# A memory norm done feature-major: statistics by a DRAM round trip, GpSimd in place of TensorE transposes

## The chip, the cores and the metric

The kernel runs on one core of a Trainium2 chip. The metric is the device time of one execution in microseconds (us). Before the change it is 1298.52 us, the median of three runs (1297.15 to 1299.23).

## The reference

Two layers of a decoder trunk on 256 tokens of width 1024, all in fp32. Cut to what matters here:

```python
def layer_norm(x, g, b):
    mu = xf.mean(-1, keepdims=True)
    var = jnp.square(xf - mu).mean(-1, keepdims=True)
    return (xf - mu) * lax.rsqrt(var + LN_EPS) * g + b

def hybrid_layer(x, mem_n, ...):
    h = layer_norm(ALPHA * x + 0.5 * swiglu(x, ffn1_w_gu, ffn1_w_down), ln_g[0], ln_b[0])
    ...
    o_xa = memory_cross_attention(xa_q, mem_n, w_mem_kv)     # k, v = split(mem_n @ w_mem_kv)
    ...

def reference(x, mem, mem_ln_g, mem_ln_b, ...):
    mem_n = layer_norm(mem, mem_ln_g, mem_ln_b)              # (256, 1024), once for both layers
    for l in range(2):
        x = hybrid_layer(x, mem_n, ...)
```

What is left out of a layer is gated DeltaNet, sliding-window attention, the gated merge with its output projection and norm, and the second SwiGLU with its norm. The product mem_n @ w_mem_kv needs mem_n with its features on the 128 partitions, as TensorE contracts over partitions.

## The kernel before

Every fp32 operand of a large product is split into a high part (ScalarE's cast to fp32r, "hi") and the rest (VectorE's subtraction, "lo"): `split`, lines 115 to 117. Weights come as one stream of units of 512 KB (`unit`, line 99): SyncE loads a unit into one of three raw buffers, ScalarE casts it into one of five whi buffers, VectorE subtracts into one of five wlo buffers. A product is then three matmuls: hi by hi, hi by lo, lo by hi (line 126 holds every matmul).

The first SwiGLU runs as *steps* f = 2 to 21 (`Ffn.rest`, line 369). A step computes 128 gate and 128 up features for all 256 tokens (`shares`, line 167): two units of weights, 32 matmuls in eight quads, two PSUM banks out of four. So a step can't begin before the banks of the step two back are read, by ScalarE's copies (L183) and VectorE's additions (L184). Then follow ScalarE's SiLU (L372 before), VectorE's product (L374 before) and a split into the tile u. After step 21 comes the down projection, then the norm of the stream, and `memory_kv` (line 448), which multiplies the normalised memory by w_mem_kv.

The norm of the memory is slipped between the steps of the first layer by `memory_T` (line 423), whose functions are called behind given steps: 11 loads gain and bias, broadcast over partitions (gB, bB); 13 and 15 load 128 memory tokens each into a tile pp, norm it on VectorE (`layernorm` with no src) and have TensorE transpose it (`to_T`: eight 128x128 transposes a tile, through PSUM), with ScalarE and VectorE splitting the result into w0 to w3; 16 writes these four tiles to DRAM (mdr), from where the second layer reads them back.

The order on each engine is set by a scheduler at build time and is then fixed: an engine runs its rows one after the other, and a row that waits holds all behind it. Loads are kept in program order on SyncE. The casts and subtractions of weight units have a priority that moves them ahead.

Of the kernel before, what the change touches and what calls it, by code (L numbers as in the profile page):

```python
# [14 lines left out]
ALU = mybir.AluOpType  # L15
AX = mybir.AxisListType

P = 128
# [19 lines left out]
@with_exitstack  # L38
def tile_trunk(ctx, tc, x, xT, mem, wst, lnp, memln, cvw, rows, cst, out):
    nc = tc.nc  # L40
# [232 lines left out]
    def layernorm(y, gB, bB, eps, src=None, fin=None, sizes=(512, 512)):  # L273
# [14 lines left out]

        if src:
            nc.scalar.activation(rs, mv[:, 1:2], AF.Sqrt, bias=epsc[:, eps:eps + 1])  # L290
            nc.vector.reciprocal(rs, rs)
            nc.vector.scalar_tensor_tensor(rt, mv[:, 1:2], epsc[:, eps:eps + 1], rs, op0=ALU.add, op1=ALU.mult)
            nc.vector.scalar_tensor_tensor(rt, rt, -0.5, rs, op0=ALU.mult, op1=ALU.mult)
            nc.vector.scalar_tensor_tensor(rs, rt, 1.5, rs, op0=ALU.add, op1=ALU.mult)
# [128 lines left out]
    def memory_T(mT, l):  # L423

        got = {}
        flat = lambda t: t.rearrange("p k t -> p (k t)")

        def again():
            mT.extend(T(pu, [P, 4, S], f"w{i}", F32R) for i in range(4))
            for i, t in enumerate(mT):  # L430
                nc.gpsimd.dma_start(flat(t), mdr[i])

        def keep():
            for i, t in enumerate(mT):
# [12 lines left out]

# [672 lines left out]
```

## Time and profile before

| | us |
|---|---|
| median of the runs | 1298.52 |
| the profiled execution, its own time | 1298.02 |
| its span in the trace | 1296.2 |
| TensorE busy | 1277.9 (99%) |
| VectorE busy | 888.4 (69%) |
| ScalarE busy | 708.5 (55%) |
| GpSimd busy | 77.2 (6%) |

In the profile PE is TensorE's matmuls, PEld its weight loads, DVE VectorE, ACT ScalarE, POOL GpSimd, SP SyncE. A row of a timeline gives the start, the length, the engine, the source line and operation, what is written <- what is read, and in brackets the idle time before it and what ended that. Times count from the start of the span. Names of tiles stand without buffer numbers: t<-acc is the pair of a step's banks being read, whi and wlo are weight units, pp the memory tile, w the four tiles of normalised memory.

### The profile page before, as it was taken

Reading aid. Unit: us, or ns where it says so; the run is one execution under the profiler, and the core shown is the slowest. Engines: PE = TensorE matmul, PEld = TensorE weight load, DVE = VectorE, ACT = ScalarE, POOL = GpSimd, SP = SyncE. Lnnn points to the kernel's source line nnn. Section 1 sums busy time; section 2 is a strip of 40 time slices with the busy share of each in tenths; the row PEclk is TensorE's granted clock in tenths of the full one; section 3 lists DMA queues with packets and bytes.
Section 4 is the critical chain, followed back from the end, with each engine's and each line's share of the span. In section 5 each row is a group of like instructions: output and inputs, shape, how many; then the busy total and the mean of one; then the engine's idle time right before and its main releaser. Section 6 shows DMA issues by size and latency. Waiting matters only on the chain.

```text
span 1296.2 us, 20444 instructions
## 1 busy us (share of the span) xinstructions
PE 1277.9 (99%) x7832; PEld 1116.2 (86%) x7832; DVE 888.4 (69%) x1430; ACT 708.5 (55%) x1177; POOL 77.2 (6%) x135
## 2 busy tenths in 40 slices
PE   8999999999999999999999999999999999999997
PEld 6888889999878888888888888899988788888886
DVE  6787556796647777665677674759867388777645
ACT  6656444666674546554455654456656654565541
POOL 0000000102311000000000000000033100000000
PEclk9999999999999999999999999999999999999999
DMA  7867564654533636555665555556453256455553
GB/s 266 276 210 244 193 229 128 220 174 135 161 131 130 228 129 211 191 185 192 228 222 200 188 186 192 199 175 201 163 165 131 98 182 224 149 194 194 189 189 111
DMA packets 68577, 240.25 MB, mean 185 GB/s; under 512 B 8160, under 2 KB 9312, under 8 KB 68480
## 3 DMA queue, kind: packets, MB, share of 16 engines
q1 hardware_dynamic: 66176, 232.53, 53.1%
q0 software_dynamic: 2304, 6.43, 1.8%
q8 instruction: 61, 1.00, 0.3%
q14 instruction: 36, 0.29, 0.1%
HBM read 235.64 MB, written 3.28 MB: 184 GB/s over the span
## 4 chain that ended last, share of the span: by engine, by line
PE 89%; DVE 4%; DMA 4%; ACT 2%; issue 1%; SPq 0%; DVEq 0%; ACTq 0%
PE acc L126 78%; PE at L126 4%; DMA raw<-in_wst_dram 3%; PE sm L126 3%; PE sm L129 1%; ACT whi L116 1%; DVE wlo L117 1%; PE acc L340 1%; PE acc L337 1%; DMA pp<-in_mem_dram 1%; PE acc L338 1%; PE at L129 1%; DVE bnst L282 0%; DVE u L117 0%; DVE h L301 0%
## 5 line engine op out<-in xcount | busy, mean ns | idle before, releaser
L117 DVE TENSOR_TENSOR wlo<-raw,whi 128x1024 fp32r<-128x1024 f32 (+2 forms) x403 | 487.4, 1214 | 308.7 <-ACT whi L116 307.2
L116 ACT CAST whi<-raw 128x1024 fp32r<-128x1024 f32 (+2 forms) x403 | 414.4, 1033 | 366.7 <-DMA raw<-in_wst_dram 99.0
L126 PE MATMUL acc<-hT,whi 128*128 128x512 f32 (+1 forms) x1952 | 524.9, 357 | 0.0
L126 PEld LDWEIGHTS acc<-hT,wlo 128*128 128x128 f32 x1616 | 304.6, 189 | 56.0
L126 PE MATMUL acc<-hT,wlo 128*128 128x256 f32 x1616 | 347.6, 279 | 0.0
L126 PEld LDWEIGHTS acc<-hT,whi 128*128 128x128 f32 x1952 | 299.8, 190 | 0.2
L126 PE MATMUL acc<-whi,u 128*128 128x512 f32 (+1 forms) x800 | 246.7, 373 | 0.0
L126 PEld LDWEIGHTS acc<-whi,u 128*128 128x128 f32 x800 | 150.1, 188 | 27.7 <-DVE t L184 1.2
L126 PE MATMUL acc<-whi,hT 128*128 128x512 f32 (+1 forms) x544 | 168.4, 380 | 5.6 <-ACT whi L116 5.6
L126 PE MATMUL acc<-wlo,u 128*128 128x512 f32 (+1 forms) x400 | 148.4, 371 | 0.0
L126 PEld LDWEIGHTS acc<-whi,hT 128*128 128x128 f32 x544 | 100.6, 189 | 23.7 <-ACT whi L116 5.6
L126 PE MATMUL acc<-wlo,hT 128*128 128x512 f32 (+1 forms) x272 | 101.9, 375 | 0.0
L126 PEld LDWEIGHTS acc<-wlo,u 128*128 128x128 f32 x400 | 75.5, 189 | 12.2
L372 ACT ACTIVATE t<-t 128x256 f32<-128x256 f32 x80 | 33.4, 417 | 60.4 <-DVE t L184 59.9
L184 DVE TENSOR_TENSOR t<-t,acc 128x256 f32<-128x256 f32 x160 | 59.9, 415 | 0.0
L126 PEld LDWEIGHTS acc<-wlo,hT 128*128 128x128 f32 x272 | 51.5, 190 | 8.2 <-DVE wlo L117 0.9
L183 ACT COPY t<-acc 128x256 f32<-128x256 f32 x160 | 51.5, 369 | 0.1
L116 ACT CAST u<-t 128x256 fp32r<-128x256 f32 x80 | 32.1, 401 | 20.4 <-DVE t L374 20.4
L374 DVE TENSOR_TENSOR t<-t 128x256 f32<-128x256 f32 x80 | 33.9, 424 | 9.2 <-ACT t L372 7.7
L126 PE MATMUL at<-whi,u 128*128 128x256 f32 x152 | 39.0, 283 | 0.0
L117 DVE TENSOR_TENSOR u<-t,u 128x256 fp32r<-128x256 f32 x80 | 33.6, 420 | 7.1 <-ACT u L116 7.1
L489 DVE SCALAR_TENSOR_TENSOR t<-acc,cw,t 128x255 f32<-128x255 f32 (+2 forms) x72 | 34.5, 479 | 0.9
(248 smaller groups left out, 1250.4 us busy)
## 6 DMA issues: line engine op xcount, KB each, us to landing
raw<-in_wst_dram SPq DMA_DIRECT2D x409, 512.0 KB, 3.6
raw<-in_wst_dram SPq DMA_DIRECT2D x16, 324.0 KB, 3.0
gB<-in_lnp_dram SPq DMA_DIRECT2D x6, 512.0 KB, 6.4
bB<-in_lnp_dram SPq DMA_DIRECT2D x6, 512.0 KB, 5.9
mdr<-w POOLq DMA_DIRECT2D x4, 512.0 KB, 6.8
w<-dr POOLq DMA_DIRECT2D x4, 512.0 KB, 8.8
w<-mdr POOLq DMA_DIRECT2D x4, 512.0 KB, 5.2
t<-in_xT_dram SPq DMA_DIRECT2D x4, 256.0 KB, 5.3
```

The lines of the kernel that those rows point to most:

```text
L116: nc.scalar.copy(hi, src)
L117: return nc.vector.tensor_tensor(lo, src, hi.bitcast(F32), op=ALU.subtract).ins
L126: return pe(nc.tensor.matmul(*a, **k))
L129: return pe(nc.tensor.transpose(*a))
L183: nc.scalar.copy(y[:, t], banks[t][:, S:])
L184: nc.vector.tensor_tensor(y[:, t], y[:, t], banks[t][:, 0:S], op=ALU.add)
L337: nc.tensor.matmul(ps, hT[0][:, k, ts], hi[:, c], start=k == 0, stop=False)
L338: nc.tensor.matmul(ps, hT[0][:, k, ts], lo[:, c], start=False, stop=False)
L340: nc.tensor.matmul(ps, hT[1][:, k, ts], hi[:, c], start=False, stop=k == KD - 1)
L372: nc.scalar.activation(y[:, 0], y[:, 0], AF.Silu)
L374: nc.vector.tensor_tensor(hf, y[:, 0], hf, op=ALU.mult)
L489: nc.vector.scalar_tensor_tensor(yc[:, j, d:], b[:, j, :S - d], w[:, t:t + 1], yc[:, j, d:], op0=ALU.mult, op1=ALU.add)
```

## The change

The host also passes the memory feature-major (memT: two halves of 512 features, each [128, 4, 256]) and gain and bias with features on partitions (128 x 2 x 8 numbers). The work behind the steps is now:

- 13 and 14: load 128 memory tokens each, take mean and variance on VectorE, and put the mean and the reciprocal root (by integer start value and three Newton steps) into two columns of a small tile mst.
- 15: GpSimd writes mst to DRAM as rows (256 means, then 256 reciprocals), in pieces of one number, and reads them back broadcast to all partitions (512 numbers each) into a tile that has gB's place.
- 17 and 18: load one half of memT each into pp, and GpSimd subtracts the mean, multiplies by the reciprocal, and applies gain and bias per feature; then `split` into w0 and w2 (first half), w1 and w3 (second half).
- 19: the four tiles are written to mdr as before.

```diff
-        if src:
-            nc.scalar.activation(rs, mv[:, 1:2], AF.Sqrt, bias=epsc[:, eps:eps + 1])
...
-        else:
-            nc.vector.tensor_scalar(mv[:, 1:2], mv[:, 1:2], LN_EPS, None, ALU.add)
-            rsqrt(rs, mv[:, 1:2], rt)
+        nc.scalar.activation(rs, mv[:, 1:2], AF.Sqrt, bias=epsc[:, eps:eps + 1])
...
         def vecs():
-            got["gb"] = gb(memln[0], memln[1])
+            got["st"] = T(pu, [P, 2, 2], "mst")
+            got["gb"] = T(pu, [P, 2, KD], "mgb")
+            load(got["gb"], memln)
             mT.extend(T(pu, [P, 4, S], f"w{i}", F32R) for i in range(4))
 
         def rows_(tb):
+
             m = T(p2, [P, D], "pp")
             load(m, mem[tb * P:(tb + 1) * P, :])
-            layernorm(m, *got["gb"], 0, None, lambda q: to_T(lambda q: (mT[q], mT[2 + q]), tb, m, q))
-
-        return {13: again} if l else {11: vecs, 13: lambda: rows_(0), 15: lambda: rows_(1), 16: keep}
+            mv = T(p3, [P, 2], "bnmv")
+            st = T(p3, [P, 4, 6], "bnst")[:, :2, :]
+            for j in range(2):
+                nc.vector.bn_stats(st[:, j, :], m[:, j * 512:j * 512 + 512])
+            nc.vector.bn_aggr(mv, st)
+            nc.vector.tensor_copy(got["st"][:, 0, tb:tb + 1], mv[:, 0:1])
+            nc.vector.tensor_scalar(mv[:, 1:2], mv[:, 1:2], LN_EPS, None, ALU.add)
+            rsqrt(got["st"][:, 1, tb:tb + 1], mv[:, 1:2], T(p3, [P, 1], "rst"))
+
+        def spread_():
+
+            d = T(pd, [2, 2, P], "ms")
+            nc.gpsimd.dma_start(d.rearrange("a t p -> p a t"), got["st"])
+            got["row"] = T(pu, [P, D], "gB")[:, 0:512]
+            nc.gpsimd.dma_start(got["row"], d.rearrange("a t p -> (a t p)").partition_broadcast(P))
+
+        def half(q):
+            m = T(p2, [P, 4, S], "pp")
+            load(m, memT_[:, q])
+            mean, rs = (got["row"][:, c:c + S].unsqueeze(1).to_broadcast([P, 4, S]) for c in (0, S))
+            nc.gpsimd.tensor_tensor(m, m, mean, op=ALU.subtract)
+            nc.gpsimd.tensor_tensor(m, m, rs, op=ALU.mult)
+            for j in range(4):
+                g, b = (got["gb"][:, n, 4 * q + j:4 * q + j + 1] for n in range(2))
+                nc.gpsimd.tensor_scalar(m[:, j], m[:, j], g, b, ALU.mult, ALU.add)
+            split(mT[q], mT[2 + q], m)
+
+        return {13: again} if l else {11: vecs, 13: lambda: rows_(0), 14: lambda: rows_(1), 15: spread_, 17: lambda: half(0), 18: lambda: half(1), 19: keep}
```

In `kernel` the host's array memT is added, and memln is reshaped to features on partitions.

The order of the rows on the engines is the same before step 11 and behind the down projection. Two places matter. The first is ScalarE's queue around steps 15 to 18. Before (t2_173 is step 15, t2_189 step 16, u7 holds steps 14 and 15; whi_206 is step 18's second unit, whi_213 and whi_216 are step 19's; sm is the PSUM tile with the second memory tile's transposes):

```order
L183 COPY t2_173_1036<-acc_165_990 128x256 [waits PE_49]
L183 COPY t2_173_1036<-acc_166_991 128x256 [waits PE_49]
L116 CAST whi_206_1224<-raw_205_1223 128x1024 [waits DMAHW3_49,PE_49,Activation_49]
L372 ACTIVATE t2_173_1036<-t2_173_1036 128x256 [waits DVE_49]
L116 CAST u7_164_987<-t2_173_1036 128x256 [waits DVE_49]
L116 CAST whi_213_1258<-raw_212_1257 128x1024 [waits DMAHW4_49,PE_49,Activation_49]
L183 COPY t2_189_1130<-acc_181_1084 128x256 [waits PE_49]
L116 CAST w0_125_780<-sm_179_1068 128x4x128 [waits PE_49]
L183 COPY t2_189_1130<-acc_182_1085 128x256
L116 CAST w1_126_781<-sm_180_1077 128x4x128 [waits PE_49]
L116 CAST whi_216_1280<-raw_215_1279 128x1024 [waits DMAHW5_49,PE_49,Activation_49]
```

Now (t2_174 is step 15, t2_185 step 16; whi_203 is step 18's second unit, whi_211 and whi_214 are step 19's; pp_196 and pp_207 are the two halves of memT):

```order
L183 COPY t2_174_1038<-acc_166_992 128x256 [waits PE_49]
L183 COPY t2_174_1038<-acc_167_993 128x256 [waits PE_49]
L116 CAST whi_203_1197<-raw_202_1196 128x1024 [waits DMAHW3_49,PE_49,Activation_49]
L368 ACTIVATE t2_174_1038<-t2_174_1038 128x256 [waits DVE_49]
L116 CAST w0_125_779<-pp_196_1162 128x1024 [waits Pool_49]
L116 CAST u7_161_968<-t2_174_1038 128x256 [waits DVE_49]
L116 CAST whi_211_1241<-raw_210_1240 128x1024 [waits DMAHW5_49,PE_49,Activation_49]
L183 COPY t2_185_1097<-acc_177_1051 128x256 [waits PE_49]
L183 COPY t2_185_1097<-acc_178_1052 128x256 [waits PE_49]
L116 CAST w1_126_780<-pp_207_1228 128x1024 [waits Pool_49]
L116 CAST whi_214_1263<-raw_213_1262 128x1024 [waits DMAHW6_49,PE_49,Activation_49]
```

The casts into w0 and w1 are now one of 1024 columns each, wait for GpSimd where they waited for TensorE, and the emptying of step 16's banks (t2_185<-acc_177 and acc_178) stands between them, behind the first. On VectorE the remainders into w2 and w3 stand at the corresponding places: w2 behind step 15's product and ahead of step 16's additions, w3 ahead of step 17's.

The second place is the head of GpSimd's queue. Before, it has nothing to do until the tiles are written to mdr (w0 to w3 are the four tiles):

```order
L435 DMA mdr_1_100<-w0_125_780 128x1024 [waits Activation_49]
L435 DMA mdr_1_100<-w1_126_781 128x1024 [waits Activation_49]
L435 DMA mdr_1_100<-w2_127_782 128x1024 [waits DVE_49]
L435 DMA mdr_1_100<-w3_128_783 128x1024 [waits DVE_49]
L747 MEMSET w0_471_2855 32x8x32 [waits DMASW0_49,PE_49]
L746 MEMSET w1_472_2856 128x1024 [waits DMASW1_49,PE_49]
```

Now the trip and the arithmetic come first (ms is the DRAM tile, mst the statistics, gB the broadcast rows, mgb gain and bias):

```order
L455 DMA ms_175_1047<-mst_123_776 128x4x1 [waits DVE_49]
L457 DMA gB_176_1049<-ms_175_1047 128x512 [waits DMASW0_49]
L463 ISA
L463 TENSOR_TENSOR pp_196_1162<-pp_196_1162,gB_176_1049 128x1024 [waits DMAHW7_49,DMAHW1_49,DMASW1_49]
L464 TENSOR_TENSOR pp_196_1162<-pp_196_1162,gB_176_1049 128x1024 [waits Pool_49]
L463 TENSOR_TENSOR pp_207_1228<-pp_207_1228,gB_176_1049 128x1024 [waits DMAHW4_49,DMAHW2_49]
L467 TENSOR_SCALAR pp_196_1162<-pp_196_1162,mgb_124_777 128x256 [waits Pool_49]
L467 TENSOR_SCALAR pp_196_1162<-pp_196_1162,mgb_124_777 128x256 x3
L464 TENSOR_TENSOR pp_207_1228<-pp_207_1228,gB_176_1049 128x1024 [waits Pool_49]
L467 TENSOR_SCALAR pp_207_1228<-pp_207_1228,mgb_124_777 128x256 [waits Pool_49]
L467 TENSOR_SCALAR pp_207_1228<-pp_207_1228,mgb_124_777 128x256 x3
```

GpSimd's third wide operation, on the second half, stands ahead of the small ones of the first half. On SyncE the second memory tile's load moves from behind step 15's units to behind step 14's, the 512 KB loads of gB and bB for the memory are replaced by one of 8 KB, and the loads of memT's halves stand behind the units of steps 17 and 18. The first load of gB for the stream's own norm now waits for GpSimd.

More of the change, by code (lines that the diff above doesn't have):

```diff
@@ L38, in tile_trunk @@
 @with_exitstack
-def tile_trunk(ctx, tc, x, xT, mem, wst, lnp, memln, cvw, rows, cst, out):
+def tile_trunk(ctx, tc, x, xT, mem, memT_, wst, lnp, memln, cvw, rows, cst, out):
     nc = tc.nc
@@ L1101 @@
         "mem": i["mem"][0],
+        "memT": np.ascontiguousarray(i["mem"][0].T.reshape(2, 4, P, S).transpose(2, 0, 1, 3)),
         "wst": _stream(i),
         "lnp": np.stack([i["ln_g"], i["ln_b"]], 2),
[L1104 removed]
+        "memln": np.ascontiguousarray(np.stack([i["mem_ln_g"], i["mem_ln_b"]]).reshape(2, KD, P).transpose(2, 0, 1)),
         "cvw": np.ascontiguousarray(i["dn_conv_w"].reshape(NL, 4, 12, P).transpose(3, 0, 2, 1)),
```

9 lines of the change are left out of this document (4 added, 5 removed).

## The prediction

> **What bounds the kernel now.** I read the page's busy times first, then its chain of waits, then the windows around the memory's norm, then the timeline of TensorE there. The two first lines of the next fence are the page's; the last two are windows (start:end, length, then busy us and count of PE, PEld, DVE, ACT and POOL, the granted clock, DMA share and GB/s).
>
> ```profile
> PE 1277.9 (99%) x7832; PEld 1116.2 (86%) x7832; DVE 888.4 (69%) x1430; ACT 708.5 (55%) x1177; POOL 77.2 (6%) x135
> PE 89%; DVE 4%; DMA 4%; ACT 2%; issue 1%; SPq 0%; DVEq 0%; ACTq 0%
> 85.00:90.00 5.00, 3.87 (x24) 3.27 (x23) 4.89 (x10) 2.65 (x6) 0.00 (x0) 1.00 0.46 159
> 170.00:196.00 26.00, 26.00 (x145) 22.56 (x144) 16.66 (x26) 10.35 (x11) 0.00 (x0) 1.00 0.69 229
> ```
>
> TensorE is busy 99% of the span and carries 89% of the chain. So an edit is worth what it adds to or takes from TensorE's own queue, or the holes that it opens or closes there. One hole lies in the first layer's memory norm: TensorE is busy 3.87 of 5 us from 85 to 90. From 170 to 196, just before the next stage, it is full, so a hole opened earlier isn't made good there.
>
> The timeline of TensorE (start, length of the merged piece, matmuls, and in brackets the idle time before it) has the norm's four groups of transposes. I quote the first and the rows that stand around each.
>
> ```profile
> 86.16 0.63 PE L126 MATMUL acc<-hT,whi 128*128 128x512 f32 x2
> 86.86 0.63 PE L126 MATMUL acc<-hT,whi 128*128 128x512 f32 x2
> 88.85 0.66 PE L129 MATMUL sm<-cs,pp 128*128 128x128 f32 x4 [1.13 <-DVE pp L301]
> 89.26 0.71 PE L126 MATMUL acc<-hT,whi 128*128 128x512 f32 x2
> 93.54 0.63 PE L126 MATMUL acc<-hT,whi 128*128 128x512 f32 x2
> 94.85 0.63 PE L126 MATMUL acc<-hT,whi 128*128 128x512 f32 x2
> 105.31 0.63 PE L126 MATMUL acc<-hT,whi 128*128 128x512 f32 x2
> 106.78 0.63 PE L126 MATMUL acc<-hT,whi 128*128 128x512 f32 x2
> 107.92 0.63 PE L126 MATMUL acc<-hT,whi 128*128 128x512 f32 x2
> ```
>
> A quad (two whi matmuls, two wlo) repeats every 0.70 us, and a step of the first half of the SwiGLU has eight quads: 5.6 us. From 86.86 to 89.26 a quad took 2.40, from 93.54 to 94.85 1.31, from 105.31 to 106.78 1.47, from 106.78 to 107.92 1.14. Over 0.70 each, that is 1.70 + 0.61 + 0.77 + 0.44 = **3.5 us** for sixteen transposes and the 1.13 us in which TensorE waited for VectorE.
>
> **What the change removes.** All 3.5 us go, since no transpose is left and TensorE waits for nothing of the norm directly. By the order of TensorE's rows, two quads of step 14 stand ahead of the first transposes, so step 14 begins at 86.16. With nothing in the way, steps 15 to 19 begin at 91.8, 97.4, 103.0, 108.6 and 114.2 on this clock. VectorE loses eight 512-wide operations of the norm; that lies under TensorE and I cost it at nothing, the cover being TensorE's own 5.6 us a step.
>
> **What it adds: a chain that must end before ScalarE arrives.** The new chain is statistics on VectorE, a trip to DRAM, and GpSimd; ScalarE's cast into w0 waits for its end, at a fixed place of ScalarE's queue. I follow it on the clock above.
>
> *Statistics.*
>
> ```profile
> 69.00 8.73 SPq L110 DMA_DIRECT2D raw<-in_wst_dram  x4
> 72.54 1.28 DVE L282 BATCH_NORM_STATS2 bnst<-pp 128x6 f32<-128x512 f32 x2
> 77.64 0.74 DVE L184 TENSOR_TENSOR t<-t,acc 128x256 f32<-128x256 f32 x2
> 80.67 0.16 DVE L269 SCALAR_TENSOR_TENSOR rst<-rstd 128x1 f32<-128x1 f32 x1
> 80.87 0.16 DVE L270 TENSOR_TENSOR rst<-rst,bnmv 128x1 f32<-128x1 f32 x1
> DMA to landing us min/median/max: 5.2/6.2/7.3
> ```
>
> SyncE's queue sends four weight units between 69.00 and 77.73, and before the change the second memory tile stands behind the fourth. Now it stands behind the second, so it goes out at about 72 and lands 6.2 later (5.2 to 7.3) at 78.4: just as VectorE is through with step 11's additions (77.64 + 0.74). From there to the last row of the statistics the order has 32 rows on VectorE: two bn_stats (1.28), three wlo subtractions, two products, two casts' remainders and a pair of additions, and 21 operations on one column.
>
> ```profile
> 113.40 1.23 DVE L117 TENSOR_TENSOR wlo<-raw,whi 128x1024 fp32r<-128x1024 f32 x1 [0.53 <-ACT whi L116]
> 114.54 0.74 DVE L184 TENSOR_TENSOR t<-t,acc 128x256 f32<-128x256 f32 x2
> 117.13 0.42 DVE L374 TENSOR_TENSOR t<-t 128x256 f32<-128x256 f32 x1
> 118.02 0.42 DVE L117 TENSOR_TENSOR u<-t,u 128x256 fp32r<-128x256 f32 x1 [0.47 <-ACT u L116]
> 75.03 1.05 ACT L116 CAST whi<-raw 128x1024 fp32r<-128x1024 f32 x1 [1.42 <-PE acc L126]
> 112.00 0.41 ACT L116 CAST u<-t 128x256 fp32r<-128x256 f32 x1 [1.31 <-DVE t L374]
> 112.31 1.05 ACT L116 CAST whi<-raw 128x1024 fp32r<-128x1024 f32 x1
> 113.27 0.63 ACT L183 COPY t<-acc 128x256 f32<-128x256 f32 x2
> ```
>
> By these rows of a quiet step (VectorE: wlo, pair of additions, product, remainder; ScalarE: small cast, whi cast, pair of copies; a wlo is followed after 1.14, a small cast after 0.31, a whi after 0.96) the wide ones are 1.28 + 3.42 + 0.84 + 0.84 + 0.74 = 7.1. A one-column operation takes 0.20 to the next where it depends on it (80.67 to 80.87), and under 0.1 where it doesn't; with 0.13 as the middle, 21 are 2.8. So the statistics are complete at 78.4 + 9.9 = **88.3**, 2 us either way.
>
> *The trip.* It has no row of its own, for nothing before moves four-byte pieces. The nearest are the other trip through DRAM and a broadcast of rows.
>
> ```profile
> 315.94 0.60 POOL L726 DMA_DIRECT2D dr<-t  x1
> 319.55 1.22 POOL L730 DMA_DIRECT2D w<-dr  x2 [3.00 <-DMA dr<-t]
> w<-dr POOLq DMA_DIRECT2D x4, 512.0 KB, 8.8
> rw<-in_rows_dram SPq DMA_DIRECT2D x1, 144.0 KB, 4.1
> t<-in_xT_dram SPq DMA_DIRECT2D x4, 256.0 KB, 5.3
> ```
>
> There GpSimd issues a 64 KB write at 315.94 and can issue the read back at 319.55: 3.6. The new write is 512 pieces of 4 bytes; I add 1.0 as an estimate (nothing below, 5.2 above, which is w<-dr's 8.8 less 3.6). The read back is 256 KB broadcast, between rw's 4.1 (144 KB) and t's 5.3 (256 KB): 4.7, with 3.0 (the landing of that 64 KB write) and 8.8 as ends. The rows stand in all partitions at 88.3 + 4.6 + 4.7 = **97.6**; the ends are 95 and 106. The two halves of memT are there by then or soon: the first goes out behind step 17's second unit at about 90 and lands at 96, the second behind step 18's at about 95 and lands at 101, before the third of GpSimd's operations needs it.
>
> *GpSimd.*
>
> ```profile
> L936 POOL TENSOR_TENSOR u<-u,gt 128x512 f32<-128x512 f32 x8 | 10.3, 1288 | 63.6 <-DVE gt L933 63.6
> L744 POOL TENSOR_TENSOR w<-t,cs 128x256 f32<-128x256 f32 x2 | 1.5, 740 | 0.2
> L738 POOL COPY t<-cs 128x128 f32<-128x128 f32 x2 | 0.6, 289 | 0.1
> 233.99 1.29 POOL L476 TENSOR_TENSOR u<-u,rw 128x512 f32<-128x512 f32 x1 [12.50 <-ACT u L473]
> 234.07 1.23 DVE L555 TENSOR_TENSOR spt<-ba,rw 128x8 f32<-128x8 f32 x1
> 287.44 0.17 DVE L574 TENSOR_TENSOR g<-spp,nea 128x8 f32<-128x8 f32 x1
> ```
>
> A tensor_tensor takes 1.29 at 512 and 0.74 at 256, so 2.39 at 1024. A tensor_scalar of 256 is not shown; between a copy of 128 (0.29) and that tensor_tensor of 256 I take 0.45. Three wide and four small ones stand ahead of w0's data: 7.2 + 1.8 = 9.0. But the last rows show that GpSimd and VectorE keep each other out: an 8-column VectorE operation with two SBUF inputs, begun 0.08 after a GpSimd one, took 1.23 and ended with it, where such an operation takes 0.17 otherwise. In that time VectorE has two wlo subtractions to do; each goes between two GpSimd operations, 2 × 1.2. So w0's data are ready at 97.6 + 9.0 + 2.4 = **109.0**. [...]
>
> *ScalarE.* Its row ahead of w0 is the cast of step 18's second unit, which waits, as whi has five buffers, until TensorE has left the first unit of step 16: 97.4 + 2.8 = 100.2 (the row at 75.03 is such a cast, step 14's first, released as step 11 ends). With the SiLU that follows ScalarE stands at w0 by 101.7. It then idles 7.3 us. Queued behind w0 are a cast of step 15, step 19's first weights, and the two copies that empty step 16's banks. Those two banks are step 18's; until ScalarE and then VectorE have read them TensorE can't begin step 18. VectorE's own queue stands too: its remainder into w2 waits for the cast.
>
> After 109.0: casts and copies take 1.05 + 0.31 + 0.96 + 0.63 on ScalarE. On VectorE the remainder into w2 could start at 110.1, but GpSimd's fourth wide operation holds it until 111.4; then w2 1.2, u 0.34, wlo 1.14, additions 0.74, with two small GpSimd operations between: 0.9. Step 18 begins at **115.7**, where 108.6 was due. Meanwhile GpSimd, held up in turn by w2, u and wlo (2.7), ends at 109.0 + 2.4 + 1.8 + 2.7 = 115.9. ScalarE's cast into w1 waits for that, and ahead of the emptying of step 17's banks stand the cast (1.05), then on VectorE w3, wlo, product, wlo, u and the additions (1.14 + 1.14 + 0.42 + 1.14 + 0.42 + 0.74): step 19 begins at 115.9 + 6.05 = **121.9**, where 114.2 was due. The loss is 7.7 us, and later steps follow at TensorE's pace, as VectorE and ScalarE have time to spare in them.
>
> *The rest.*
>
> ```profile
> 110.00:115.00 5.00, 5.00 (x31) 4.38 (x30) 3.68 (x7) 2.69 (x7) 0.37 (x1) 1.00 1.01 379
> 119.47 1.05 ACT L116 CAST whi<-raw 128x1024 fp32r<-128x1024 f32 x1 [1.49 <-DMA raw<-in_wst_dram]
> ```
>
> The four tiles' write to mdr filled the DMA engines (share 1.01 from 110 to 115) and held a weight cast for 1.49, while TensorE stayed at 5.00 of 5 on the units cast ahead. It moves to about 117 to 125, and I cost it at nothing under the same cover; if that is gone, 1.5. Two 512 KB vectors less and two 512 KB halves more leave the bytes as they were. The first gB load gains a wait for GpSimd on SyncE's queue; it stood at 177, 60 us after GpSimd is done, so nothing. The second layer reads mdr as before.
>
> **The sum.** The profiled execution took 1298.02 (span 1296.2); the median of the runs is 1298.52. 1298.02 − 3.5 + 7.7 = 1302.2; I forecast **1302**.
>
> **Rivals.**
> 1. *The chain ends in time; faster.* With the lower ends everywhere (statistics 86.3, rows at 93, memT's second half at 100.2, small operations of 0.29, no mutual exclusion) w0 is ready at 100.2 + 2.4 + 1.2 = 103.8, w1 at 107.4, and step 19 could begin at 113.4, under its 114.2. ScalarE waits 2 us and TensorE none: 1298.0 − 3.5 = **1294.5**. It decides when w0's data come before about 104 (without exclusion) or 101 (with it). For it speaks that TensorE has two steps of weights and a free pair of banks when ScalarE stops; against it, that every term must be at its lower end.
> 2. *No exclusion, the rest as forecast.* w0 at 97.6 + 9.0 = 106.6, step 19 at 106.6 + 4.2 + 6.05 = 116.9, a loss of 2.7: **1297.2**. The row at 234.07 speaks against it.
> 3. *A slow trip or a slow start.* With the trip's upper end, 106, w0 is ready at 117 and step 19 begins at 130: a loss of 16, **1310**. GpSimd's first arithmetic could also start late by itself: an ISA row now stands behind the broadcast's issue, where before it lay in an idle stretch of 12.5 us ahead of 233.99, so the trace bounds it only by 0 and 12.5. [...]
>
> **How the numbers follow.** The forecast (a loss of 4.5 to 10.5, so 1299 to 1305) gets 0.50, rival 1 with losses up to 1.5 gets 0.12, rival 2 with losses of 1.5 to 4.5 gets 0.16, rival 3 (1305 to 1312) 0.22. A measurement of this kernel tells some 0.2% from no change, 2.6 us: faster is under 1295.9, slower over 1301.1. Faster is nearly all of rival 1, 0.11; rival 2 and the lower third of the forecast are the same, 0.34; the rest is slower, 0.55. The range 1296 to 1308 leaves out rival 1 and the upper third of rival 3, together 0.19.
>
> **What would show it.** In the profile after: no L129 matmuls from pp; the idle of ScalarE before w, released by POOL, 7 us and again some before the second w; TensorE idle at two step starts, released by VectorE's additions, 7.7 in all between 108 and 122; a wide GpSimd operation near 2.4, and longer where VectorE is at work. I am wrong if TensorE has no hole there (rival 1), if the rows land far from 97.6, or if a hole appears at step 14, where VectorE's wait for the second memory tile would be to blame.

## The result, and where the time went

The changed kernel takes **1318.44 us** (median of 4 runs, 1317.45 to 1320.77), the kernel before 1297.97 beside it (median of 4, 1297.15 to 1299.23): a ratio of 1.0159 (95% interval 1.0142 to 1.0177), slower by about 20 us. The forecast was 1302, with a range of 1296 to 1308. The side was right; the size was not.

The profiled execution of the change took 1317.45 (span 1315.5). The first lines of its page are busy time by engine and shares of the chain that ended last.

```profile
PE 1286.1 (98%) x7816; PEld 1118.8 (85%) x7816; DVE 887.1 (67%) x1422; ACT 708.4 (54%) x1175; POOL 97.0 (7%) x149
PE 85%; DMA 5%; DVE 4%; ACT 3%; issue 1%; POOL 1%; SPq 0%; DVEq 0%; ACTq 0%; POOLq 0%
```

TensorE has 16 matmuls less and is called busy 8 us longer, and the chain has lost 4 points of TensorE to DMA, ScalarE and GpSimd. The timeline of TensorE from 103 to 130 shows both the holes and why a smaller number of matmuls can be busy for longer (start, length, matmuls, idle time before).

```profile
103.81 0.40 PE L126 MATMUL acc<-hT,wlo 128*128 128x256 f32 x2
111.79 1.22 PE L126 MATMUL acc<-hT,whi 128*128 128x512 f32 x2 [7.58 <-DVE t L184]
113.23 1.05 PE L126 MATMUL acc<-hT,whi 128*128 128x512 f32 x2
114.52 1.05 PE L126 MATMUL acc<-hT,whi 128*128 128x512 f32 x2
115.80 0.63 PE L126 MATMUL acc<-hT,whi 128*128 128x512 f32 x2
...
124.56 1.22 PE L126 MATMUL acc<-hT,whi 128*128 128x512 f32 x2 [5.11 <-DVE t L184]
...
129.68 0.63 PE L126 MATMUL acc<-hT,whi 128*128 128x512 f32 x2
```

There are two large holes, 7.58 and 5.11 us long. And behind each of them TensorE is slow: a pair of whi matmuls takes 1.05 in place of 0.63. Three quads go from 111.79 to 115.80, 4.01 us where three take 2.09 at 0.70 each (1.9 lost); four go from 124.56 to 129.68, 5.12 for 2.79 (2.3 lost). The windows name the cause; their columns are start:end, length, busy us and count of PE, PEld, DVE, ACT and POOL, then granted clock, DMA share and GB/s.

```profile
90.00:95.00 5.00, 5.00 (x32) 4.38 (x31) 3.30 (x6) 3.26 (x6) 0.00 (x0) 1.00 0.79 63
95.00:100.00 5.00, 5.00 (x31) 4.38 (x30) 1.07 (x3) 0.00 (x0) 0.49 (x1) 1.00 0.76 31
105.00:110.00 5.00, 0.00 (x0) 0.00 (x0) 1.59 (x3) 2.37 (x5) 2.02 (x1) 0.90 0.98 376
110.00:115.00 5.00, 3.21 (x10) 2.78 (x11) 5.00 (x5) 0.99 (x2) 4.92 (x3) 0.50 0.38 113
125.00:130.00 5.00, 5.00 (x18) 4.28 (x18) 2.84 (x4) 3.36 (x5) 3.20 (x6) 0.55 0.87 321
```

The clock granted to TensorE is 0.50 from 110 to 115 and 0.55 from 125 to 130, where it is 1.00 from 90 to 100. The first two rows show something else: from 90 to 100 the DMA engines are busy 0.79 and 0.76 of the time, and move 63 and 31 GB/s. GpSimd and ScalarE in that stretch:

```profile
88.95 0.97 POOL L455 DMA_DIRECT2D ms<-mst  x1 [88.11 <-DVE mst L271]
99.51 0.57 POOL L457 DMA_DIRECT2D gB<-ms  x1 [9.59 <-DMA ms<-mst]
107.98 2.34 POOL L463 TENSOR_TENSOR pp<-pp,gB 128x1024 f32<-128x1024 f32 x1 [7.90 <-DMA gB<-ms]
110.40 3.24 POOL L464 TENSOR_TENSOR pp<-pp,gB 128x1024 f32<-128x1024 f32 x1
113.59 3.38 POOL L463 TENSOR_TENSOR pp<-pp,gB 128x1024 f32<-128x1024 f32 x1
102.63 1.05 ACT L116 CAST whi<-raw 128x1024 fp32r<-128x1024 f32 x1 [7.93 <-DMA raw<-in_wst_dram]
108.04 1.04 ACT L116 CAST whi<-raw 128x1024 fp32r<-128x1024 f32 x1 [2.33 <-DMA raw<-in_wst_dram]
119.33 1.04 ACT L116 CAST w<-pp 128x1024 fp32r<-128x1024 f32 x1 [7.15 <-POOL pp L467]
126.08 1.04 ACT L116 CAST w<-pp 128x1024 fp32r<-128x1024 f32 x1 [3.91 <-POOL pp L467]
```

The small write goes out at 88.95 and GpSimd waits 9.59 for it; the rows are there at 107.98. Meanwhile ScalarE waits 7.93 and 2.33 for weights, which has nothing to do with GpSimd's arithmetic, and only from 112 on for GpSimd's results (7.15 and 3.91). VectorE's additions, for which TensorE waits in the first hole, stand behind the cast at 108.04 and behind a remainder that took 2.29 beside GpSimd's first operation, where 1.23 is usual; so about 1 of the 7.58 us is that. The list of transfers in the window from 86 to 110 (KB each, median us from issue to landing) shows who shared the DMA engines with the small write:

```profile
raw<-in_wst_dram SPq DMA_DIRECT2D x5, 512.0 KB, 12.7
pp<-in_memT_dram SPq DMA_DIRECT2D x2, 512.0 KB, 15.0
gB<-ms POOLq DMA_DIRECT2D x1, 256.0 KB, 8.4
ms<-mst POOLq DMA_DIRECT2D x1, 2.0 KB, 10.3
```

Two kilobytes took 10.3 us to land, and the 512 KB units of weights behind them 12.7. The page of before has this for all weight units of that size, and the eight of the same window took 3.5:

```profile
raw<-in_wst_dram SPq DMA_DIRECT2D x409, 512.0 KB, 3.6
```

Not all of the loss stands there. The activation that begins a norm of the stream can be found in both traces, first behind the down projection and last at the end.

```profile
192.23 0.29 ACT L290 ACTIVATE rstd<-bnmv,epsc 128x1 f32<-128x1 f32 x1 [2.88 <-DVE bnmv L285]
1289.82 0.29 ACT L290 ACTIVATE rstd<-bnmv,epsc 128x1 f32<-128x1 f32 x1 [7.59 <-DVE bnmv L285]
```

The same two rows after the change:

```profile
207.88 0.29 ACT L289 ACTIVATE rstd<-bnmv,epsc 128x1 f32<-128x1 f32 x1 [3.84 <-DVE bnmv L285]
1308.65 0.30 ACT L289 ACTIVATE rstd<-bnmv,epsc 128x1 f32<-128x1 f32 x1 [7.66 <-DVE bnmv L285]
```

The change is 15.7 us late at the first and 18.8 at the last: 3.2 us more are lost in 1100 us in which the order of instructions is the same as before, and no hole is to be seen.

So the sum for the profiled execution is: -3.5 (the sixteen transposes), 7.6 + 5.1 + 0.3 (holes), 1.9 + 2.3 (half clock behind them), 3.2 (later), and 1.0 in the first 33 us: 17.9 of the 19.4 us. The 1.0 need be no work of the change: an activation at 32.62 before and 33.58 after stands at 33.61 in a1, which has the order of before up to step 14, and at 32.72 and 33.08 in j1 and j4, which have all of it.

### The profile page after: what moved, and what is told of

The parts are those of the page before. It is cut to its first block, busy times and chain, and to the rows that moved or that the text cites. A ratio compares the mean times of both kernels' runs of the same rounds, so it can differ in the third digit from the quotient of the medians.

```text
span 1315.5 us, 20414 instructions
## 1 busy us (share of the span) xinstructions
PE 1286.1 (98%) x7816; PEld 1118.8 (85%) x7816; DVE 887.1 (67%) x1422; ACT 708.4 (54%) x1175; POOL 97.0 (7%) x149
## 3 DMA queue, kind: packets, MB, share of 16 engines
HBM read 235.91 MB, written 3.28 MB: 182 GB/s over the span
## 4 chain that ended last, share of the span: by engine, by line
PE 85%; DMA 5%; DVE 4%; ACT 3%; issue 1%; POOL 1%; SPq 0%; DVEq 0%; ACTq 0%; POOLq 0%
PE acc L126 75%; PE at L126 4%; DMA raw<-in_wst_dram 3%; PE sm L126 3%; ACT whi L116 1%; PE sm L129 1%; DVE wlo L117 1%; DMA ms<-mst 1%; DVE u L117 1%; DMA gB<-ms 1%; PE acc L336 1%; PE acc L333 1%; PE at L129 0%; PE acc L334 0%; POOL pp L463 0%
```

## The experiments

Theory 1 was that the small write, by its 512 pieces, is the cause of the first hole and of all that follows. Theory 2 was the prediction's own: GpSimd's arithmetic stands directly ahead of ScalarE's cast. Theory 3 came with the fifth run (the mutual exclusion of GpSimd and VectorE costs by itself), theory 4 with the late loss. "Before" beside each group had a median of 1296.8, 1297.8, 1297.2, 1297.5 and 1297.7; where runs of two groups are compared below, each is also taken against its own. The medians of j1 and k128 count one execution of 4491 us each; without it they are 1300.16 and 1298.97.

| run | what it is | median us | ratio to before, 95% interval |
|---|---|---|---|
| a1 | before, with the small write | 1305.41 | 1.0073 (1.0055 to 1.0092) |
| b1 | change, 16-byte pieces | 1311.22 | 1.0109 (1.0093 to 1.0126) |
| c1 | change without the trip | 1307.80 | 1.0084 (1.0069 to 1.0099) |
| d1 | change, halves in steps 20 and 21 | 1313.24 | 1.0125 (1.0108 to 1.0142) |
| e1 | 16-byte pieces, casts apart | 1305.95 | 1.0064 (1.0051 to 1.0078) |
| e2 | 4-byte pieces, casts apart | 1309.72 | 1.0092 (1.0078 to 1.0105) |
| g2 | without the trip, on VectorE | 1299.48 | 1.0012 (1.0003 to 1.0021) |
| g1 | 16-byte pieces, on VectorE | 1304.74 | 1.0055 (1.0042 to 1.0069) |
| e3 | as e1, operations in quarters | 1298.83 | 1.0014 (1.0005 to 1.0023) |
| e4 | as e3, scale and shift on ScalarE | 1300.18 | 1.0021 (1.0011 to 1.0030) |
| i1 | as e4, tiles at the old addresses | 1295.59 | 0.9989 (0.9980 to 0.9998) |
| h1 | before, with the added input | 1297.16 | 1.0000 (0.9992 to 1.0009) |
| j1 | before, tiles at the new addresses | 1300.51 | 1.0023 (1.0014 to 1.0032) |
| j2 | change, tiles at the old addresses | 1313.99 | 1.0129 (1.0115 to 1.0143) |
| j3 | as e3, tiles at the old addresses | 1295.51 | 0.9984 (0.9976 to 0.9993) |
| j4 | before, tiles shifted by 96 bytes | 1301.48 | 1.0029 (1.0018 to 1.0040) |
| k64 | before, shifted by 64 bytes | 1300.87 | 1.0023 (1.0013 to 1.0033) |
| k128 | before, shifted by 128 bytes | 1299.03 | 1.0015 (1.0006 to 1.0024) |

### a1: the small write alone

```diff
+        def write_():                       # behind step 14 of the kernel before
+            st = T(pu, [P, 2, 2], "mst")
+            nc.vector.tensor_copy(st.rearrange("p a t -> p (a t)"), got["m"][:, 0:4])
+            d = T(pd, [2, 2, P], "ms")
+            nc.gpsimd.dma_start(d.rearrange("a t p -> p a t"), st)
```

> The kernel before, with nothing of the change but the small write: in step 14 VectorE copies four columns of the normalised first memory tile, and GpSimd's queue writes them to DRAM as 512 pieces of 4 bytes, in the layout of the change. Nobody reads them. Theory 1 (the small write blocks the DMA engines and starves the weight stream, and TensorE's hole in step 17 comes from that): the write takes about 10 us to land, the memory's second tile or the weights behind it come late, and TensorE loses 7.6 us of idle time and 1.9 of slow clock: 1307.5, from 1303 to 1310. Theory 2 (the loss comes from ScalarE standing at its casts into w0 and w1 for GpSimd's arithmetic; the write is harmless): 1298, as before.

Measured: 1305.41, 8.6 us over before. Three rows: TensorE's hole, ScalarE's wait, the write's landing.

```profile
111.04 1.12 PE L129 MATMUL sm<-cs,pp 128*128 128x128 f32 x4 [5.46 <-DVE pp L301]
107.49 1.04 ACT L116 CAST whi<-raw 128x1024 fp32r<-128x1024 f32 x1 [6.31 <-DMA raw<-in_wst_dram]
ms<-mst POOLq DMA_DIRECT2D x1, 2.0 KB, 10.0
```

A write that nobody reads makes ScalarE wait 6.31 for weights, VectorE 5.22 for ScalarE, and TensorE 5.46 for VectorE behind it. Theory 1 holds for the first hole. How the write holds up the loads is not shown: from 104 to 105, as the write landed (94.32 + 10.0), the DMA engines moved 29 GB/s here and were called busy 0.29 of the time, where the change, during its write, had 31 to 63 GB/s at 0.76 to 0.79.

### b1: the same write in 128 pieces of 16 bytes

```diff
-            d = T(pd, [2, 2, P], "ms")
-            nc.gpsimd.dma_start(d.rearrange("a t p -> p a t"), got["st"])
+            d = T(pd, [P, 2, 2], "ms")
+            nc.gpsimd.dma_start(d, got["st"])
```

> The change with another layout of the small DRAM tile: partition by partition, so that the write is 128 pieces of 16 bytes in place of 512 of 4, and GpSimd's two wide operations read the broadcast rows with a stride of four elements. The read back stays 2 KB to each partition. Theory 1: the write lands in 3 to 4 us, the weights come in time, the hole of step 17 is gone with its slow clock (9.5 us), and the later holes stay or shrink: 1300 to 1309. Theory 2: the end of GpSimd's arithmetic moves by some 6 us only if the trip does; if the size of the pieces does not matter, the time stays 1318.

Measured: 1311.22, 2 over theory 1's range; it is 14.4 over before, where the change is 20.5 over. The landing of write and read back, ScalarE's wait for GpSimd and TensorE's one hole there:

```profile
ms<-mst POOLq DMA_DIRECT2D x1, 2.0 KB, 3.9
gB<-ms POOLq DMA_DIRECT2D x1, 256.0 KB, 6.6
112.88 1.04 ACT L116 CAST w<-pp 128x1024 fp32r<-128x1024 f32 x1 [8.17 <-POOL pp L469]
118.60 1.22 PE L126 MATMUL acc<-hT,whi 128*128 128x512 f32 x2 [8.36 <-DVE t L184]
```

The write lands in 3.9, the rows are there at 99.9, and the hole of step 17 is gone. What was hidden behind it comes out: ScalarE stands 8.17 at w0, and TensorE 8.36 at step 18. That is the mechanism of the prediction, without the narrow write. It is not quite the change's arithmetic: reading the rows with a stride, GpSimd's wide operations took 2.85 to 3.87, where the change's took 2.34 to 3.38, so that w0's data came 12.9 us behind the rows and not 11.3.

### c1 and g2: no trip; GpSimd or VectorE

```diff
-            nc.gpsimd.dma_start(d.rearrange("a t p -> p a t"), got["st"])
...
-            nc.gpsimd.dma_start(got["row"], d.rearrange("a t p -> (a t p)").partition_broadcast(P))
+            nc.gpsimd.memset(got["row"], 1.0)          # g2: and nc.vector for nc.gpsimd in half()
```

> The change without its trip through DRAM: neither the small write nor the broadcast read; the row tile is filled with ones by GpSimd, so the memory is not normalised. All of GpSimd's arithmetic, the order on ScalarE and the loads of memT stay. GpSimd can begin when the first half of memT has landed, at about 97. Theory 1: no hole in step 17; w0 is ready at 97 + 9 + 1 to 2 of mutual exclusion = 107 to 108, ScalarE waits 5 us, and TensorE loses at most the prediction's later part, 0 to 7 us with its slow clock: 1295 to 1302. Theory 2: the holes behind w0 and w1 stay as they are, and most of the loss with them: 1310 or more.

> The run without the trip (row tile filled with ones, the memory not normalised), with the same arithmetic on VectorE in place of GpSimd, the places of loads and casts unchanged. Theory 2 (GpSimd's 8.4 us per half, ahead of a cast that ScalarE reaches 2 us after the half has landed, make the holes): VectorE does a half in 2 x 1.14 and four narrow operations of about 0.3, 3.5 us, ScalarE waits 1 to 3 us, and TensorE hardly at all: 1295 to 1299, where the same with GpSimd took 1307.8. Rival (the load of memT in the weights' queue makes the hole, whoever does the arithmetic): 1304 to 1308.

Measured: 1307.80 and 1299.48. In c1 GpSimd begins at 94.59, as the first half lands, and still:

```profile
94.59 2.71 POOL L461 TENSOR_TENSOR pp<-pp,gB 128x1024 f32<-128x1024 f32 x1 [93.29 <-DMA pp<-in_memT_dram]
102.99 1.05 ACT L116 CAST w<-pp 128x1024 fp32r<-128x1024 f32 x1 [6.33 <-POOL pp L465]
109.30 1.22 PE L126 MATMUL acc<-hT,whi 128*128 128x512 f32 x2 [5.50 <-DVE t L184]
```

From GpSimd's start to the cast are 8.4 us, ScalarE waits 6.33 of them, and TensorE loses 5.50. Done by VectorE in the same places the time is 8.3 us less (1.7 over before, where c1 is 11.0 over), and TensorE shows one hole of 1.0, at 136. So theory 1 is not the whole: without any trip more than half of the loss is still there, because the half lands 2 us before ScalarE asks for it and GpSimd needs 8.4. The rival for g2, that the load in the weights' queue makes the hole, falls.

### d1: the halves three steps later

```diff
-15: spread_, 17: lambda: half(0), 18: lambda: half(1), 19: keep}
+15: spread_, 20: lambda: half(0), 21: lambda: (half(1), keep())}
```

> The change with the two halves moved from steps 17 and 18 to steps 20 and 21, and the four writes to mdr behind them. The trip stays where it is. Theory 1: the write still holds up the weights, so the hole of step 17 stays with its slow clock (9.5 us), although no load of memT stands in the queue there now, and the waits for GpSimd go: 1318.4 - 7.7 = 1310.7, from 1304 to 1312. Theory 2: ScalarE no longer stands at w0 and w1, and the gain of the sixteen transposes is left: 1295 to 1298.

Measured: 1313.24; neither theory's number. The holes of TensorE:

```profile
107.58 0.90 PE L126 MATMUL acc<-hT,whi 128*128 128x512 f32 x2 [4.10 <-DVE t L184]
132.11 1.22 PE L126 MATMUL acc<-hT,whi 128*128 128x512 f32 x2 [5.87 <-DVE t L184]
```

The write's hole stays (4.10; that it is shorter because no load of memT stands in the queue is likely, not shown), and the second moves with the halves, since load, arithmetic and cast stay together. Moving the whole group later only moves its hole. Whether distance inside the group helps is what e1 asks.

### g1: the change with 16-byte pieces, arithmetic on VectorE

The edit is b1 with `nc.vector` for `nc.gpsimd` in `half`.

> The change with 16-byte pieces in the write and the arithmetic on VectorE, the casts in the change's places. VectorE now stands at the first operation until the rows have landed (99.9 in the run with 16-byte pieces) and then works 3.5 us a half without exclusion: w0's data at 103.4 in place of 112.8, w1's soon after. Theory 2: the hole of 8.4 us shrinks to 1 to 4 us and the slow clock with it: 1297 to 1302. Rival (the wait for the rows is what counts, wherever the arithmetic is done): 1306 or more, for all of VectorE's queue now stands behind that wait.

Measured: 1304.74, between the two. Where TensorE stood in this run, and what the wide operations took on VectorE with the stride, is not shown.

### e1 and e2: the casts set apart from the arithmetic

```diff
-            split(mT[q], mT[2 + q], m)
+            got[q] = m
+
+        def put_(q):
+            with tc.issue_after(held[1]):        # behind this step's last cast on ScalarE
+                split(mT[q], mT[2 + q], got[q])
...
+15: spread_, 16: lambda: half(0), 17: lambda: half(1), 20: lambda: put_(0), 21: lambda: (put_(1), keep())}
```

> The change with both suspected causes taken away: the small write in 128 pieces of 16 bytes, and GpSimd's arithmetic set apart from ScalarE's casts: the halves of memT are loaded and worked on in steps 16 and 17, and the casts into w0 and w1 stand in ScalarE's queue behind step 20's and step 21's last cast. By the run with 16-byte pieces the rows are there at 99.9, and 16.8 us of operations, stretched by the mutual exclusion, end by 120; ScalarE comes to the casts at about 130. Theory 1 and theory 2 together (write and place of the casts are all there is): no hole in TensorE, and the prediction's 3.5 us are gained: 1294.5, from 1293 to 1297. If the mutual exclusion of GpSimd and VectorE costs by itself, VectorE comes late with its additions in steps 17 to 19 and TensorE shows holes there: over 1298.

> As the run with both causes taken away, but with the write of the change, 512 pieces of 4 bytes. Theory 1: only the write's block is left: a hole in TensorE at step 16 or 17 of 4 to 8 us and 1.5 to 2 of slow clock behind it, 1300 to 1304.5. Theory 2: the write costs nothing where nobody stands at GpSimd's result: 1294.5.

Measured: 1305.95 and 1309.72. e2 is over both numbers that were expected, and 3.8 over e1: that is the narrow write's price here, perhaps too low, as GpSimd's wide operations took 2.9 on the mean in e2 and 3.4 in e1, where they read the rows with a stride. But e1, with both causes taken away, is 8 us slower than before. ScalarE no longer waits for GpSimd; VectorE's rows and TensorE's hole say what is left:

```profile
104.46 0.74 DVE L185 TENSOR_TENSOR t<-t,acc 128x256 f32<-128x256 f32 x2
105.12 3.28 DVE L118 TENSOR_TENSOR wlo<-raw,whi 128x1024 fp32r<-128x1024 f32 x1
108.32 3.13 DVE L371 TENSOR_TENSOR t<-t 128x256 f32<-128x256 f32 x1
111.92 2.55 DVE L118 TENSOR_TENSOR u<-t,u 128x256 fp32r<-128x256 f32 x1 [0.47 <-ACT u L117]
115.99 1.22 PE L127 MATMUL acc<-hT,whi 128*128 128x512 f32 x2 [4.83 <-DVE t L185]
```

A remainder that takes 1.23, a product of 256 columns that takes 0.42 and a remainder of 256 columns that takes 0.42 (the prediction's rows of a quiet step) last 3.28, 3.13 and 2.55, one behind the other, while GpSimd works without a pause from 100.5 to 122. The additions of 104.46, which take one operand from PSUM, keep the 0.74 of a quiet step. This is theory 3.

### e3 and e4: the wide operations in quarters

```diff
-            nc.gpsimd.tensor_tensor(m4, m4, mean, op=ALU.subtract)
-            nc.gpsimd.tensor_tensor(m4, m4, rs, op=ALU.mult)
+            for j in range(4):
+                m2 = m[:, j].rearrange("p (t s) -> p t s", t=2)
+                nc.gpsimd.tensor_tensor(m2, m2, mean, op=ALU.subtract)
+                nc.gpsimd.tensor_tensor(m2, m2, rs, op=ALU.mult)
```

e4 also takes the scale and shift from GpSimd:

```diff
-                nc.gpsimd.tensor_scalar(m[:, j], m[:, j], g, b, ALU.mult, ALU.add)
+                    nc.scalar.activation(m[:, j], m[:, j], AF.Identity, bias=b, scale=g)    # in put_
```

> The run with the small write in 16-byte pieces and the casts set apart, which still lost 8 us and showed one hole of 4.8 us with GpSimd at work in two-and-a-half-microsecond operations all around it. Here each wide operation is done in four of 256 columns, the work itself unchanged. Theory 3 (the mutual exclusion: each VectorE operation with two SBUF inputs waits out one GpSimd operation, so 2.3 us, and now 0.6): VectorE gets 1.14 of every 1.75 us, 65 per cent, where TensorE's pace needs 3.8 of every 5.6, 68 per cent, so the hole all but goes: 1294.5 to 1300. Rival (VectorE loses GpSimd's busy time however it is cut, about 14 us against a slack of 1.8 us a step): the hole stays at 4 us or more, 1304 to 1307.

> As the run in quarters, with the scale and shift by feature moved from GpSimd to ScalarE: four operations of 256 columns ahead of each cast into w0 and w1, about 0.42 each. GpSimd's time falls from 14 to 9.4 us, ScalarE's rises by 3.4 in steps 21 and 22, where it has 2 us of 5 to spare. Theory 3: no hole, and the rest as in the run in quarters or 1 to 2 us better: 1294 to 1299. Rival (GpSimd's busy time is lost however it is cut): a hole of 0 to 3 us, 1297 to 1303.

Measured: 1298.83 and 1300.18. VectorE's weight remainders and products from 100 to 122, by shape (count, busy us, mean ns), first with whole operations, then in quarters:

```profile
L118 DVE TENSOR_TENSOR wlo<-raw,whi 128x1024 fp32r<-128x1024 f32 x5 | 9.6, 1911 | 1.7 <-ACT whi L117 1.7
L371 DVE TENSOR_TENSOR t<-t 128x256 f32<-128x256 f32 x2 | 3.5, 1771 | 0.0
```

```profile
L118 DVE TENSOR_TENSOR wlo<-raw,whi 128x1024 fp32r<-128x1024 f32 x8 | 11.1, 1384 | 2.6 <-ACT whi L117 2.6
L371 DVE TENSOR_TENSOR t<-t 128x256 f32<-128x256 f32 x4 | 4.3, 1085 | 0.0
```

The same work of GpSimd, cut four times finer, gives the remainder back half a microsecond (1911 to 1384 ns) and lets eight of them through where five went, and the hole of 4.83 is gone, although GpSimd is now at it for 29 us (98.2 to 127.6) and not 22. The time is 1.6 over before where e1 was 8.1 over: 6.5 us for one edit. Theory 3 is shown, and its rival (GpSimd's busy time is lost however it is cut) falls. Moving the scale to ScalarE brought nothing more; why e4 is not faster than e3 stays open.

### i1 and h1: the late loss

```diff
+            T(pu, [P, D], "gB"), T(pu, [P, D], "bB")          # i1: places kept as before
-            got["st"] = T(pu, [P, 2, 2], "mst")
-            got["gb"] = T(pu, [P, 2, KD], "mgb")
+            got["st"] = T(p3, [P, 2, 2], "mst", bufs=1)
+            got["gb"] = T(p3, [P, 2, KD], "mgb", bufs=1)
```

```diff
-            load(m, mem[tb * P:(tb + 1) * P, :])
+            load(m, memT_[:, tb].rearrange("p k t -> p (k t)"))          # h1, in the kernel before
```

> As the run with the scale and shift on ScalarE, with the tiles of the memory and of the mixers at the SBUF addresses of before (the change moves w0 to w3, u6 to u13, gB and bB by up to 45 KB). All profiles of the change and of its variants lose 2 to 4 us more between 192 us and the end, in small steps, and the run with the small write alone loses none. Theory 4a (the places of the tiles do that): 2 to 4 us less than the run with the scale and shift on ScalarE. Theory 4b (the added input in DRAM, or the smaller number of instructions, or chance): the same time within 1 us.

> The kernel before with one more input in DRAM, the feature-major memory of the change; its norm reads its two 512 KB tiles from there, so it normalises the wrong values, in the same time. Theory 4b, DRAM side (the added input moves the weights in DRAM, and that costs 2 to 4 us in the later stages): 1300 to 1302. Theory 4a or chance: 1297.8, as before.

Measured: 1295.59, 4.6 under e4, and 1297.16, as before. The change allots two small tiles ahead of the large ones in SBUF, and gB and bB later than before; that moves all the tiles behind them. The input in DRAM does nothing.

### j1, j2, j3, j4, k64, k128: addresses alone

j2 and j3 have the edit of i1; the others only allot tiles that are not used:

```diff
             # j1, ahead of the norm's gain and bias in the kernel before
+            T(pu, [P, 2, 2], "mst"), T(pu, [P, 2, KD], "mgb")
             mT.extend(T(pu, [P, 4, S], f"w{i}", F32R) for i in range(4))
+            for t in ("u6", "u7", "gB", "u8", "u9", "u10", "u12", "u13", "bB"):
+                T(pu, [P, D], t)
             got["gb"] = gb(memln[0], memln[1])
             # j4
+            T(pu, [P, 2, 2], "mst"), T(pu, [P, 2, KD], "mgb")
             # k64 and k128, n of 64 and 128
+            T(pu, [P, n // 4], "pad")
```

> The kernel before, instruction for instruction, with its tiles in SBUF at the addresses of the change (w0 to w3 8 KB lower, u6 and u7 8 KB lower, u8 to u10, u12 and u13 4 KB lower, gB and bB behind them, all shifted by 96 bytes). Theory 4a (the addresses alone cost 3 to 4.6 us in the later stages): 1300 to 1302. Theory 4b (they cost nothing by themselves): 1297.2, as before.

> The change, instruction for instruction, with its tiles at the SBUF addresses of before. Theory 4a: 1318.4 less 3 to 4.6: 1314 to 1315.5. Theory 4b: 1318.4.

> The run in quarters (16-byte pieces, casts set apart, wide operations in four) with its tiles at the SBUF addresses of before. Theory 4a: 1298.8 less 3 to 4.6: 1294.2 to 1295.8, that is the prediction's 3.5 us of sixteen transposes less what is left of the hole. Theory 4b: 1298.8.

> The kernel before with all tiles behind u5 shifted by 96 bytes, as in the change, their order kept. If the shift itself costs (theory 4a, by alignment): 1300 to 1302. If it is the new neighbourhood of the tiles (theory 4a, by the distances of 4 and 8 KB): 1297.2, and the kernel with its tiles moved alone shows the loss.

> The kernel before with all tiles behind u5 shifted by 128 bytes, their order kept. If the offset within 128 bytes (or within 64 or 32) is what counts: 1297.5, as before, and the streaming matmuls at 391 to 397 ns. If any shift against the first tiles costs: 1300.5 to 1301.5.

> The same with a shift by 64 bytes. If the offset within 64 bytes counts: 1297.5. If the offset within 128 bytes counts, or any shift costs: 1300.5 to 1301.5.

Measured: the kernel before is 3.0 slower with its tiles moved, 4.0 with a mere shift by 96 bytes, 3.2 with 64 and 1.3 with 128; the change is 4.5 faster with its tiles at the old places (4.0 when each is taken against its own before). In j2 the two activations of the late loss stand 15.7 and 15.1 behind before, so none is left there. Theory 4a holds in both directions, and it is the shift and not the new neighbours. TensorE's groups show it; first before (count, busy us, mean ns):

```profile
L126 PE MATMUL acc<-whi,u 128*128 128x512 f32 x648 | 219.3, 395 | 0.0
L126 PE MATMUL acc<-whi,w 128*128 128x512 f32 x88 | 29.1, 397 | 0.7 <-DVE w L117 0.7
L126 PE MATMUL acc<-wlo,w 128*128 128x512 f32 x44 | 17.2, 391 | 0.0
```

then before with the shift of 96 bytes:

```profile
L126 PE MATMUL acc<-whi,u 128*128 128x512 f32 x648 | 221.1, 397 | 0.0
L126 PE MATMUL acc<-whi,w 128*128 128x512 f32 x88 | 29.6, 402 | 1.1 <-DVE w L117 0.6 <-ACT w L116 0.5
L126 PE MATMUL acc<-wlo,w 128*128 128x512 f32 x44 | 17.5, 397 | 0.0
```

A 512-wide matmul with u or w takes 2 to 6 ns longer. Over the five such groups (acc<-wlo,u and acc<-u,w are the other two) the busy time grows by 3.6 us with 96 bytes, 2.9 with 64, 2.3 with 128; in the change it had grown by 3.5, and in j2 it is back within 0.2. That busy time is a sign and not a price: in a1, which allots the 16 bytes of mst, it grows by 1.6, and nothing is lost behind 192. No shift that was tried is free, so which property of the address counts stays open.

j3 is the fastest kernel of the study: 1295.51 against 1297.51 beside it, 2 us or 0.16%, and its interval (0.9976 to 0.9993) does not reach 1.

## Why the prediction was wrong, step by step

- **What bounds the kernel, what the change removes.** Right. In j3 the activation at 192 comes 3.6 us earlier than before, counted from the activation at 32.6, in i1 3.9, in e3 3.0, where 3.5 was forecast. But 3.5 is what one execution had to give: the 1.13 us in which TensorE waited for VectorE are not in the traces of j1 and k128 (0.2 and 0.1 us idle ahead of those transposes), and in j1 the same stretch is 1.1 us shorter than before. The medians of j3 and i1 are 2.0 and 1.6 under before.
- **Statistics, complete at 88.3.** Right: GpSimd, which waited for VectorE's last row of them, issues the write at 88.95.
- **The trip, rows at 97.6.** This is the step that failed. Its term "512 pieces of 4 bytes; I add 1.0 (nothing below, 5.2 above)" was mis-sized: from the write's issue to the read's are 10.6 us, not 4.6, and the upper end of 8.8 didn't hold it either. The read back took 8.4 for 4.7. The rows came at 108.0, far from 97.6, which the prediction named as a sign of being wrong. With 16-byte pieces they came at 99.9 (b1), so it is the number of pieces that the estimate from a 64 KB write could not see.
- **What the trip does to others.** Not in the prediction at all: the DMA engines were counted as a path with a duration, not as a thing that the weights need too. The first hole is in step 17, a step ahead of the forecast, with the weights as its cause; ScalarE came to w0 at 112.2, not at 101.7, and the halves of memT landed 15.0 after issue (median), not 6. a1 shows that price without the rest of the change: 8.6 us.
- **GpSimd, 11.4 us from the rows to w0's data.** Right: 11.3 (107.98 to 119.3). A wide operation took 2.34 at 107.98 (2.39 was forecast), the next two 3.24 and 3.38 (with 1.9 for the exclusion in all, where 2.4 was forecast), and a small one 0.58 for the 0.45 of the estimate: the sum came out nearer than its terms, and that is luck. The late first start of rival 3 cost nothing: the first operation begins 0.07 after the rows have landed (99.51 + 8.4). Whether a late start lies under the 7.90 us for which GpSimd waited for the rows is not shown.
- **ScalarE waits 7.3 at w0 and again at w1.** Right in kind: 7.15 and 3.91. c1 and b1 show that this mechanism alone makes a hole of 5.5 to 8.4.
- **Later steps follow at TensorE's pace.** Wrong, for two reasons that the sum lacked. Behind the holes of 7.58 and 5.11 TensorE's granted clock was 0.50 and its matmuls slow for 4 to 5 us: 4.2 us lost in all here. The same 0.50 stands behind holes of 5.50 (c1), 4.10 (d1) and 2.14 (e2), for 3 to 5 us; behind holes of 1.01 (g2) and 1.13 (before) the granted clock stayed at 1.00. And the addresses cost 3 to 4.5.
- **mdr costs nothing, the gB load nothing.** Right within 0.3 (the only hole of TensorE near it has 0.25, at 138).
- **The rivals.** The nearest was the slow trip, 1310 at 0.22: rows at 106 for the 108 that came. Its price for TensorE was too low by the weights, the clock and the addresses. b1, with its rows at 99.9, says about what a trip of the forecast length would have given: 1311, and the forecast would still have been 9 short, the half clock (2.3) and the addresses (3 to 4.5) making some 6 of them.

So the direction came out of the right mechanism, and most of the size out of what was not in the sum. The profiled execution took 15.2 us more than the 1302.2 of the sum: 5.3 in the holes (13.0 for 7.7), 4.2 by the half clock, 3.2 later, by the addresses, 1.0 in the first 33 us, and 1.5 that are open. That GpSimd and VectorE exclude each other was in it, as two waits of 1.2; by e1 and e3 it is worth 6.5 us once nothing else hides it. In e1 VectorE's rows took 2.55 to 3.28 beside GpSimd operations of 3.4 on the mean.

What stays open: 1.5 of the 19.4 us; how a write of 2 KB holds up the loads of another queue; why the granted clock falls behind a hole of 2.14 us and not behind one of 1.13; why e4 is no faster than e3; and what in an address makes a matmul 2 to 6 ns longer.

## What to carry to other kernels

Price a small transfer by its pieces and by who else needs the DMA engines in that time, not by its bytes: here 2 KB took 10.3 us in 512 pieces and 3.9 in 128. Put distance between a slow engine's result and the in-order queue that will stand at it (ScalarE's stood 7.15 and 3.91 us), and cut what GpSimd does beside a busy VectorE into short operations (6.5 us from e1 to e3). Where a change allots a tile, look whether it has moved the others (1.3 to 4.0 us), and on a kernel bound by TensorE charge each hole of a few microseconds something for the clock (1.9 and 2.3 us behind the holes of 7.58 and 5.11).

## What the runs showed of the hardware

- Writes of 2 KB in 512 pieces of 4 bytes from GpSimd's queue landed after 10.3, 10.0, 10.0 and 9.5 us (the change, a1, d1, e2), in 128 pieces of 16 bytes after 3.9, 3.1 and 3.1 (b1, e1, e3) and 1.9 (e4, i1). While the one of the change ran, the DMA engines, with 512 KB loads on another queue, moved 31 to 63 GB/s and were called busy 0.76 to 0.79 of the time; in a1, from 104 to 105, 29 GB/s at 0.29.
- After holes of 2.14, 4.10, 5.50, 5.11 and 7.58 us TensorE's granted clock was 0.50 for 3 to 5 us of work (e2, d1, c1, and two in the change); after holes of 1.01 and 1.13 (g2, before) it stayed at 1.00.
- VectorE's operations with two SBUF inputs took 2.29 to 3.28 us beside GpSimd's wide ones, where they take 0.42 or 1.23; its additions with an operand in PSUM kept their 0.74 (the change, e1).
- Shifting the tiles behind u5 by 64, 96 or 128 bytes costs a kernel of 1297 us 3.2, 4.0 and 1.3 us (k64, j4, k128), and its 512-wide matmuls that read the shifted tiles are busy 2.9, 3.6 and 2.3 us longer.
